# One change to the recurrence of a two-layer decoder: A blocks on half the rows of the matrix array, one head at a time

## The chip, the core and the metric

The kernel runs on one core of a Trainium2 chip. Five engines work side by side, each through its own list of instructions in order: TensorE (PE in the profile; its weight loads are listed apart as PEld), VectorE (DVE), ScalarE (ACT), GpSimd (POOL), and SyncE (SP), which here only issues DMA transfers. They wait for each other through semaphores. Matrix products write to PSUM, from which VectorE and ScalarE copy results to SBUF. The metric is the time of one execution in microseconds (us) on the device; lower is better.

## The reference, cut to what matters

The model has a layer with an RWKV-7 mixer and an MLP, shared keys and values, and a second layer with forgetting attention and an MLP, on 1024 tokens of width 1024, all in float32. The change is in the recurrence of the RWKV-7 mixer, which the reference writes token by token for each of 16 heads with 64 features:

```python
    def step(S, inp):
        r_t, w_t, k_t, v_t, kk_t, b_t = inp
        sa = jnp.einsum('bhvk,bhk->bhv', S, -kk_t)
        S = (S * w_t[:, :, None, :] + sa[..., None] * b_t[:, :, None, :]
             + v_t[..., None] * k_t[:, :, None, :])
        y_t = jnp.einsum('bhvk,bhk->bhv', S, r_t)
        return S, y_t
    ...
    mean = jnp.mean(y, axis=-1, keepdims=True)
    var = jnp.mean(jnp.square(y - mean), axis=-1, keepdims=True)
    y = (y - mean) * lax.rsqrt(var + GN_EPS)
    ...
    bonus = jnp.sum(r_h * k_h * r_k.astype(f32), axis=-1, keepdims=True) * v_h
    y = (y + bonus.reshape(B, T, D)).astype(h.dtype) * g
    return y @ w_o
```

## The kernel before, in words

The kernel does the recurrence in 16 chunks of 64 tokens. Within a chunk everything is a matrix product; between chunks only the state goes on. The 16 heads are 8 pairs, with one head of a pair on partitions 0 to 63 and the other on 64 to 127. An earlier stage scales kk, r, b and k with the decays and writes them to DRAM, by chunk (`d_KR`, `d_BK`).

What a chunk needs:

- *A blocks* (`rec_blocks`). For each head, the products of b and k (64 tokens each) with kk and r (64 tokens each) over the head's 64 features, masked to the causal part. `BK[:, p]` holds b and k of pair p, both heads, on 128 partitions. `KRz` holds kk and r of the pair so that the columns of one head are zero on the other head's partitions. One product per pair of 128 x 128 weights with 256 columns then gives the blocks of both heads. Two pairs fill a PSUM tile `ap`; VectorE multiplies it with the mask into `AE` (L416). There are four such tiles in a chunk. TensorE shows a float32 product as two weight loads and two matmuls, so four products are eight records.
- *Token-major b and k* (`rec_turn`): eight transposes into two tiles `tp`, copied by ScalarE to `BKt` (L425).
- *Inverse of the triangular system* (`rec_load_blocks`, `rec_corner`, `rec_corner2`): diagonal blocks are loaded (`B11`, `BT2`, `TT`), and the corner is made by the small products `op` and `op2`. `rec_corner` also writes kk, scaled to the chunk before, to `AE` (VectorE, L444) and scales r in place (GpSimd, L444).
- *Solve, state, output* (`rec_solve`, `rec_state`, `rec_out`): `pp` (from AE and Z, which holds the state beside v), copied to `Ps` by ScalarE; `yp` starts the output with r and the state; `sa`, scaled into Z by VectorE (L475); `u` gives the next state (VectorE L489, GpSimd `St` L494); a second `yp` adds the rest of the output.
- *Norm and gate* (`rec_norm`, `rec_gate`): VectorE takes `m` (L517, L518) and `Y` (L519) from `yp`, ScalarE the squares, and so on; one chunk later the product `zp` and the gate follow.

Chunk c does its solve, state and output, while the A blocks, transposes and corner of chunk c + 1 are made in between: part "a" of `prepare` (the first half of the A blocks) before `rec_state`, part "b" (the second half, and the transposes) after `rec_out`. From chunk 3 on, `fill` puts 24 products of the output projection (`wo`) into each chunk. In the first chunks `hook` puts in the last product of the gate (`gp`) and the loads and splits of w_o.

What sets the order: TensorE takes the recurrence's products in the order of the program (`Pinned`). The other engines' lists are made at build time by a scheduler that simulates the program, and may stand in another order than the code.

Buffers that matter: `ap`, `tp`, `op`, `op2` and `zp` share the PSUM pool `psA`, which has three buffers, taken in turn; a tile waits until the one three before it has been read. The A blocks of part "b" and the two `tp` follow each other, so the second `tp` waits for the copy of the first `ap` tile of part "b". `KRz` has two places (even and odd chunks), `BK` has one: the load of the next BK waits for the transposes of the present one.

Of the kernel before, what the change touches and what calls it, by code (L numbers as in the profile page):

```python
# [8 lines left out]
F32 = mybir.dt.float32  # L9
# [7 lines left out]
P = 128  # L17
# [12 lines left out]
# the recurrence's start: chunk of the first load of x; steps of the gate's product at each of its places;  # L30
# first place of a load of w_o, places between two loads, places from a load to its split
# [9 lines left out]
# engines of the steps where one stage follows another (v: VectorE, s: ScalarE, p: GpSimd), tile by tile.  # L41
# mlp_in (m), queries and keys (q): normalised x by tokens (n), its blocks from PSUM (r), the parts' forms (t, w.f),
# high parts (h) and low parts (l); products of rows (o: mlp_out, w: attention's w_o): the first and the last eighth
# of the rows (0, 9), parts of both sides (a, b), forms (f); ENG_O: the rows between
# [31 lines left out]
class K:  # L76
    """State shared by the stages."""
# [17 lines left out]
def rsqrt_small(k, pool, out, x, scale, eps, tag=""):  # L95
    """out = (x * scale + eps) ** -0.5 for a small tile, refined by one Newton step."""
# [20 lines left out]
def load_cols(k, a, pool, ps, which):  # L117
    """Feature vectors as columns: k.col[name] is [128, 8]."""
# [47 lines left out]
def rwkv_keep(k):  # L166
    """What lives from the projections to the recurrence."""
# [27 lines left out]
def block_tiles(k):  # L195
    """Diagonal blocks of the next two head pairs, one to a partition."""
    k.Nb = k.pi.tile([P, 32, 32], F32, tag="Nb", name="Nb", bufs=2)
# [6 lines left out]
def prep_unit(k, p, hf):  # L204
    """Half the tokens of a head pair: decays, scaled kk, r, b, k to DRAM, inverses of A_ab's diagonal blocks."""
# [16 lines left out]
    # log decay, its sum within a chunk, the exponentials about the middle of the chunk  # L222
# [26 lines left out]
    # b before k for the first head of the pair, k before b for the second  # L249
# [7 lines left out]
    # norms of kk: 1 / max(sum of squares, 1e-24); two chunks at a time  # L257
# [13 lines left out]
    # -A_ab, transposed; its diagonal 32 x 32 blocks one to a partition  # L271
# [19 lines left out]
def prep_inverse(k, b):  # L291
    """Inverses of 128 unit lower triangular 32 x 32 blocks, one on each partition."""
# [16 lines left out]
def rec_pools(k, ctx, a):  # L309
# [8 lines left out]
    k.KRz, k.TT = [], []  # L318
    for i in range(2):
        with tc.issue_after(k.gate_end.ins) if i else nullcontext():  # L320
            kr = k.rz.tile([P, NK, 2, 2, C], F32, tag=f"KRz{i}", name=f"KRz{i}")
            nc.gpsimd.memset(kr, 0.0)
            k.KRz.append(kr)
            tt = k.rc.tile([P, NK, 2, C], F32, name=f"TT{i}")
            nc.gpsimd.memset(tt, 0.0)
            k.TT.append(tt)
    # mask of an A block: rows (b | k) i, columns (kk / r, t): kk where i < t, r where i <= t
# [13 lines left out]
    # scale of the state from one chunk's reference to the next one's  # L341
# [6 lines left out]
class Pinned:  # L348
    """Matrix products that the tensor engine takes in the order of the program."""
# [14 lines left out]
def rec_values(k, c):  # L364
    """[state, v] of the first head of each pair, [v, state] of the second; the state comes from the chunk before."""
# [10 lines left out]
def rec_load(k, c):  # L376
    """Chunk c of all heads: scaled kk and r, b and k."""
    nc, w = k.nc, k.rw
    KR, TT = k.KRz[c % 2], k.TT[c % 2]
    BK = k.rc.tile([P, NK, 2, C], F32, tag="BK", name="BK")  # L380
    B11 = k.rc.tile([P, NK, 32], F32, tag="B11", name="B11")
    BT2 = k.rc.tile([P, NK, 32], F32, tag="BT2", name="BT2")
    for h in range(2):
        nc.sync.dma_start(KR[HALF[h], :, h], k.d_KR[c, HALF[h]])
# [6 lines left out]
def rec_load_blocks(k, s):  # L391
    """The triangular inverses' blocks."""
# [17 lines left out]
def rec_blocks(k, s, p2):  # L410
    """The A blocks of two head pairs."""
    ap = k.psA.tile([P, 2, 256], F32, tag="psA", name="ap")
    for j in range(2):
        p = 2 * p2 + j
# [1433 lines left out]
```

## Time and profile before

| | |
|---|---|
| runs | 2953.9, 2958.09 and 2966.1 us, median 2958.09 |
| the profiled execution | span 2954.2 us from its first to its last instruction; no time of its own beside the span is given |
| busy share of the span | PE 91%, PEld 74%, DVE 76%, ACT 40%, POOL 50% |
| mean granted TensorE clock | 0.952 |
| the recurrence | its first A block starts at 523.6 us, its last solve (`pp`) at 834.8 us |
| A blocks (`ap`, L355) | 256 matmul records, 66.7 us busy |
| masking of A blocks (`AE`, L416) | 64 VectorE instructions, 42.4 us busy |

A row of the timeline has start, duration, engine, line, operation, output <- inputs, shape, and count where equal instructions follow each other; the brackets give the idle time of the engine before it and what ended it. TensorE's matmuls overlap: a row's duration runs to the end of the last one, and the start of the next row tells when TensorE was free for it. A row of the groups has the count, the busy time of the group (overlaps counted once) and the mean duration of one.

### The profile page before, as it was taken

The page shows a single profiled execution, that of the slowest core. Times are in us where ns is not written, and L with a number is a line of the kernel's source. Part 1 is how long each engine was busy: PE and PEld are TensorE (multiplying, and loading weights), DVE is VectorE, ACT ScalarE, POOL GpSimd, SP SyncE. Part 2 cuts the span into 40 slices and gives each one's busy share as a digit, 9 for nine tenths or more (in the row PEclk, how much of TensorE's full clock was granted, in tenths as well). Part 3 has the DMA queues.
Part 4 walks back from the last instruction along what each step waited for, and adds up shares of the span by engine and source line. Part 5 has one row for each costly group of instructions (what it writes and reads, how often), then busy time and mean ns, then how long its engine had stood idle before and what let it go on. Part 6 is the DMA issues. An engine that isn't in the chain of part 4 may idle for free.

```text
span 2954.2 us, 46747 instructions
## 1 busy us (share of the span) xinstructions
PE 2675.9 (91%) x17666; PEld 2171.7 (74%) x17666; DVE 2246.8 (76%) x3496; ACT 1191.8 (40%) x2243; POOL 1478.3 (50%) x1059
## 2 busy tenths in 40 slices
PE   7998788799998999899977899999986999989998
PEld 4776676677886888677766899766665788867876
DVE  7059998677768555789998868566689755599998
ACT  5364433422243333323334434467635333323431
POOL 2055553465556554565665322333266555466555
PEclk9998888999998999999998999999998999999999
DMA  3358574665412333533102222644330333342311
GB/s 115 142 177 250 162 210 116 192 167 136 116 45 80 113 107 100 199 114 114 58 15 87 93 80 79 188 123 133 87 122 8 100 107 115 129 163 93 115 58 57
DMA packets 345457, 344.63 MB, mean 117 GB/s; under 512 B 137648, under 2 KB 274080, under 8 KB 345232
## 3 DMA queue, kind: packets, MB, share of 16 engines
q1 hardware_dynamic: 344240, 339.48, 36.8%
q8 instruction: 139, 2.28, 0.3%
q0 software_dynamic: 992, 2.17, 0.2%
q14 instruction: 86, 0.70, 0.1%
HBM read 236.59 MB, written 104.99 MB: 116 GB/s over the span
## 4 chain that ended last, share of the span: by engine, by line
PE 44%; DVE 17%; issue 4%; DMA 2%; POOL 1%; ACT 1%; SPq 0%; DVEq 0%; POOLq 0%; ACTq 0%
PE mm L355 8%; PE mm L740 6%; PE mm L739 6%; PE mm L741 6%; DVE ol L706 5%; PE mm L1333 4%; PE mm L1334 4%; PE mm L1332 3%; DVE xt L1345 3%; PE s L355 3%; PE tp L358 2%; PE o L355 2%; DVE T L1303 1%; DVE xlT L706 1%; DVE T L1314 1%
## 5 line engine op out<-in xcount | busy, mean ns | idle before, releaser
L1333 PE MATMUL mm<-ol,oh 128*128 128x512 f32 x992 | 400.4, 406 | 47.2 <-DVE ol L706 40.2
L1334 PE MATMUL mm<-oh,ol 128*128 128x512 f32 x992 | 385.1, 405 | 15.2 <-DVE ol L706 14.9
L1332 PE MATMUL mm<-oh 128*128 128x512 f32 x992 | 365.5, 401 | 27.8 <-ACT oh L703 18.7
L1333 PEld LDWEIGHTS mm<-ol,oh 128*128 128x128 f32 x992 | 193.5, 195 | 103.7 <-DVE ol L706 54.5
L1199 POOL TENSOR_TENSOR z<-z 128x512 f32<-128x512 f32 x128 | 144.7, 1131 | 205.3 <-ACT z L1198 205.3
L1332 PEld LDWEIGHTS mm<-oh 128*128 128x128 f32 x992 | 191.5, 194 | 75.2 <-ACT oh L703 21.7
L1334 PEld LDWEIGHTS mm<-oh,ol 128*128 128x128 f32 x992 | 192.9, 196 | 62.3 <-DVE ol L706 22.9
L703 ACT CAST oh<-r 128x512 fp32r<-128x512 f32 x211 | 124.0, 619 | 249.8 <-PE mm L1333 192.8
L740 PE MATMUL mm<-xlT,ah 128*128 128x512 f32 x512 | 203.7, 398 | 17.1 <-DVE xlT L706 17.0
L739 PE MATMUL mm<-xhT,ah 128*128 128x512 f32 x512 | 202.4, 397 | 5.6 <-ACT xhT L703 4.6
L741 PE MATMUL mm<-xhT,al 128*128 128x512 f32 x512 | 202.3, 396 | 0.0
L706 DVE TENSOR_TENSOR ol<-r,oh 128x512 fp32r<-128x512 f32 x193 | 190.4, 1016 | 6.9 <-ACT oh L703 2.9
L1345 DVE TENSOR_TENSOR xt<-xt,mm 128x512 f32<-128x512 f32 x288 | 181.5, 676 | 7.0 <-PE mm L1334 6.9
L703 ACT CAST ah<-w 128x512 fp32r<-128x512 f32 x125 | 77.3, 621 | 177.8 <-PE mm L740 173.0
L706 POOL TENSOR_TENSOR ol<-r,oh 128x512 fp32r<-128x512 f32 x63 | 98.7, 1571 | 97.5 <-ACT oh L703 81.4
L739 PE MATMUL mm<-xhB,ah 128*128 128x512 f32 x368 | 144.1, 391 | 0.0
L740 PE MATMUL mm<-xlB,ah 128*128 128x512 f32 x368 | 143.9, 391 | 0.0
L741 PE MATMUL mm<-xhB,al 128*128 128x512 f32 x368 | 143.1, 391 | 0.0
L703 ACT CAST oh<-S 128x512 fp32r<-128x512 f32 x102 | 63.0, 621 | 184.2 <-PE mm L1333 142.7
L740 PEld LDWEIGHTS mm<-xlT,ah 128*128 128x128 f32 x512 | 98.1, 192 | 41.1 <-DVE xlT L706 20.3
L706 DVE TENSOR_TENSOR ol<-S,oh 128x512 fp32r<-128x512 f32 x102 | 112.7, 1109 | 16.6 <-ACT oh L703 12.4
L706 POOL TENSOR_TENSOR ol<-T,oh 128x512 fp32r<-128x512 f32 x58 | 93.9, 1622 | 51.1 <-ACT oh L703 32.2
(522 smaller groups left out, 7815.7 us busy)
## 6 DMA issues: line engine op xcount, KB each, us to landing
w<-in_mlp_w_in_dram SPq DMA_DIRECT2D x64, 512.0 KB
r<-d_H SPq DMA_DIRECT2D x64, 512.0 KB
r<-in_mlp_w_out_dram SPq DMA_DIRECT2D x64, 512.0 KB
d_H<-z SPq DMA_DIRECT2D x60, 512.0 KB
raw<-in_rwkv_w_rkv_dram SPq DMA_DIRECT2D x24, 512.0 KB
d_KR<-KR SPq DMA_DIRECT2D x16, 512.0 KB
KRz<-d_KR SPq DMA_DIRECT2D x32, 256.0 KB
BK<-d_BK SPq DMA_DIRECT2D x16, 512.0 KB
```

The lines of the kernel that those rows point to most:

```text
L355: return self.tc.keep_in_program_order(self.tc.nc.tensor.matmul(*args, **kw))
L358: return self.tc.keep_in_program_order(self.tc.nc.tensor.transpose(*args))
L703: nc.scalar.copy(hi, src)
L706: lo_eng.tensor_tensor(lo, src, hi.bitcast(F32), op=ALU.subtract)
L739: te.matmul(out, ah, bh, start=i == 0, stop=False)
L740: te.matmul(out, ah, bl, start=False, stop=False)
L741: te.matmul(out, al, bh, start=False, stop=i == n - 1)
L1199: nc.gpsimd.tensor_tensor(dst, dst, dst, op=ALU.mult)
L1332: te.matmul(banks[t], ah[:, ts], bh, start=i == 0, stop=False)
L1333: te.matmul(banks[t], ah[:, ts], bl, start=False, stop=False)
L1334: te.matmul(banks[t], al[:, ts], bh, start=False, stop=i == n - 1)
L1345: nc.vector.tensor_tensor(d, d, o, op=ALU.add)
```

## The change: half-row products, no padding, two places for b and k

Each head's A block becomes a product of its own: 64 rows (the head's partitions) with 128 weight columns and 128 moving columns. The two heads of a pair alternate, and go to two PSUM tiles, one for each head. `rec_blocks` now makes four pairs at once: two `ap` tiles of four pairs by one head, where there were two tiles of two pairs by two heads. The padded `KRz` becomes a tile of the same size that holds kk and r in its first half and b and k in its second, so that b and k have two places as well; the fills with zeros fall away, and kk and r come with one transfer of 512 KB in place of two of 256 KB. The product of r and the state (`yp` of `rec_solve`) takes 64 rows in place of 128. Comments and docstrings are taken out too, which moves line numbers by a few.

```diff
-    k.KRz, k.TT = [], []
+    k.KRB, k.TT = [], []
     for i in range(2):
         with tc.issue_after(k.gate_end.ins) if i else nullcontext():
-            kr = k.rz.tile([P, NK, 2, 2, C], F32, tag=f"KRz{i}", name=f"KRz{i}")
-            nc.gpsimd.memset(kr, 0.0)
-            k.KRz.append(kr)
+            kr = k.rz.tile([P, 2, T], F32, tag=f"KRz{i}", name=f"KRz{i}")
+            k.KRB.append([kr[:, j].rearrange("p (c b t) -> p c b t", b=2, t=C) for j in range(2)])
...
-    KR, TT = k.KRz[c % 2], k.TT[c % 2]
-    BK = k.rc.tile([P, NK, 2, C], F32, tag="BK", name="BK")
+    (KR, BK), TT = k.KRB[c % 2], k.TT[c % 2]
...
-    for h in range(2):
-        nc.sync.dma_start(KR[HALF[h], :, h], k.d_KR[c, HALF[h]])
+    nc.sync.dma_start(KR, k.d_KR[c])
     nc.sync.dma_start(BK, k.d_BK[c])
...
-def rec_blocks(k, s, p2):
-    ap = k.psA.tile([P, 2, 256], F32, tag="psA", name="ap")
-    for j in range(2):
-        p = 2 * p2 + j
-        k.pe.matmul(ap[:, j], s["BK"][:, p], s["KR"][:, p], start=True, stop=True)
-    k.nc.vector.tensor_tensor(s["AE"][:, 2 * p2:2 * p2 + 2].rearrange("p c h k t -> p (c h k t)"),
-                              ap.rearrange("p c f -> p (c f)"), k.mask.rearrange("p c k t -> p (c k t)"), op=ALU.mult)
+def rec_blocks(k, s, p4):
+    aps = [k.psA.tile([P, 4, 2, C], F32, tag="psA", name="ap") for _ in HALF]
+    for j in range(4):
+        for ap, hs in zip(aps, HALF):
+            k.pe.matmul(ap[:, j], s["BK"][hs, 4 * p4 + j], s["KR"][hs, 4 * p4 + j], start=True, stop=True)
+    for h, ap in enumerate(aps):
+        k.nc.vector.tensor_tensor(s["AE"][:, 4 * p4:4 * p4 + 4, h], ap, k.mask, op=ALU.mult)
...
-                eng.tensor_tensor((AE, KR)[i][hs, :, h, i], KR[hs, :, h, i], sc, op=ALU.mult)
+                eng.tensor_tensor((AE[hs, :, h, 0], KR[hs, :, 1])[i], KR[hs, :, i], sc, op=ALU.mult)
...
-                k.pe.matmul(yp[hs, p], s["KR"][:, p, h, 1, :], Z[:, p, h, :], start=p == 0, stop=False)
+                k.pe.matmul(yp[hs, p], s["KR"][hs, p, 1, :], Z[hs, p, h, :], start=p == 0, stop=False)
...
             if "a" in parts:
                 rec_blocks(k, s, 0)
                 hook()
+                hook()
+            if "b" in parts:
                 rec_blocks(k, s, 1)
                 hook()
-            if "b" in parts:
-                rec_blocks(k, s, 2)
-                hook()
-                rec_blocks(k, s, 3)
                 hook()
                 rec_turn(k, s, 0)
                 hook()
```

How the order of the instructions moves is shown at three places. The first is TensorE in a chunk in the middle of the recurrence, before (KRz is kk and r, BK is b and k, and ap is an A block):

```order
L355 MATMUL pp<-Z,AE 64x64 x16
L355 MATMUL yp<-Z,KRz_4508 64x64 x16
L355 MATMUL sa<-Ps,TT_4510 64x64 x16
L355 MATMUL ap<-KRz_4512,BK 128x256 x4
L355 MATMUL u<-Z,BKt 64x64 x16
L355 MATMUL yp<-Z,AE 64x64 x16
L355 MATMUL ap<-KRz_4512,BK 128x256 x4
L358 MATMUL tp<-ident,BK 128x128 x8
```

And TensorE in the same chunk now:

```order
L354 MATMUL pp<-Z,AE 64x64 x16
L354 MATMUL yp<-Z,KRz_4508 64x64 x16
L354 MATMUL sa<-Ps,TT_4509 64x64 x16
L354 MATMUL ap<-KRz_4511 128x128 x8
L354 MATMUL u<-Z,BKt 64x64 x16
L354 MATMUL yp<-Z,AE 64x64 x16
L354 MATMUL ap<-KRz_4511 128x128 x8
L357 MATMUL tp<-ident,KRz_4511 128x128 x8
```

The order of the groups is the same; each group of A blocks is eight products of 128 columns in place of four of 256.

The second place is VectorE's list in such a chunk, from the solution Z to the variance, before:

```order
L475 TENSOR_TENSOR Z_5740<-sa_6055,ns2_96 64x8x64 x2
L416 TENSOR_TENSOR AE_6002<-ap_6074,mask_4516 128x512
L416 TENSOR_TENSOR AE_6002<-ap_6078,mask_4516 128x512
L489 TENSOR_TENSOR Z_6014<-u_6082,St_5827 64x8x64 x2
L517 TENSOR_REDUCE m_6144<-yp_6038 128x8
L518 TENSOR_SCALAR m_6144<-m_6144 128x8
L416 TENSOR_TENSOR AE_6002<-ap_6120,mask_4516 128x512
L519 TENSOR_TENSOR Y_6143<-yp_6038,m_6144 128x512
L416 TENSOR_TENSOR AE_6002<-ap_6124,mask_4516 128x512
L523 TENSOR_REDUCE var_6150<-ysq_6148 128x8
```

And now:

```order
L472 TENSOR_TENSOR Z_5766<-sa_6087,ns2_96 64x8x64 x2
L414 TENSOR_TENSOR AE_6034<-ap_6106,mask_4514 128x4x128
L414 TENSOR_TENSOR AE_6034<-ap_6107,mask_4514 128x4x128
L486 TENSOR_TENSOR Z_6046<-u_6118,St_5857 64x8x64 x2
L514 TENSOR_REDUCE m_6184<-yp_6070 128x8
L515 TENSOR_SCALAR m_6184<-m_6184 128x8
L516 TENSOR_TENSOR Y_6183<-yp_6070,m_6184 128x512
L414 TENSOR_TENSOR AE_6034<-ap_6156,mask_4514 128x4x128
L414 TENSOR_TENSOR AE_6034<-ap_6157,mask_4514 128x4x128
L520 TENSOR_REDUCE var_6190<-ysq_6188 128x8
```

The masking of part "b" has moved: Y stood between its two instructions, and now stands ahead of both.

The third place is SyncE's list of transfers at the start of the recurrence, before (d_B and d_T are the last inverses, d_g the gate; KRz of buffer 4508 serves chunks 0 and 2, that of 4512 chunk 1; BK_4699 is b and k of chunk 1):

```order
L306 DMA d_B_105<-Tb_1213 128x1024
L305 DMA d_T_104<-Tm_1214 128x1024
L399 DMA B11_4536<-d_B_105 32x8x32 x2
L1073 DMA d_g_64<-xt0_4562 128x2x512
L401 DMA BT2_4537<-d_T_104 32x8x32 x2
L405 DMA TT0_4510<-d_T_104 32x8x32 x4
L1073 DMA d_g_64<-xt1_4580 128x2x512
L405 DMA TT1_4514<-d_T_104 32x8x32 x3
L1073 DMA d_g_64<-gs_4598 128x2x512
L405 DMA TT1_4514<-d_T_104 32x8x32
L384 DMA KRz0_4508<-d_KR_98 64x8x128
L385 DMA BK_4699<-d_BK_99 128x1024
```

And now, a little earlier in the list, from b and k of chunk 0 on (buffer 4508 again serves chunks 0 and 2, 4511 chunk 1):

```order
L382 DMA KRz0_4508<-d_BK_99 128x1024
L381 DMA KRz1_4511<-d_KR_98 128x1024
L382 DMA KRz1_4511<-d_BK_99 128x1024
L339 DMA lnw_4520<-in_rwkv_lnx_w_dram 64x8x64 x2
L339 DMA lnb_4521<-in_rwkv_lnx_b_dram 64x8x64 x2
L369 DMA Z_4539<-d_v_65 64x8x64 x2
L369 DMA Z_4719<-d_v_65 64x8x64 x2
L510 DMA Vh_4851<-d_v_65 64x8x64 x2
L1068 DMA d_g_64<-xt0_4566 128x2x512
L1068 DMA d_g_64<-xt1_4580 128x2x512
L381 DMA KRz0_4508<-d_KR_98 128x1024
L306 DMA d_B_105<-Tb_1213 128x1024
```

b and k of chunk 1 have moved from behind the loads of TT to the very start, and kk and r of chunk 2 from behind the loads of TT to ahead of d_B. Elsewhere the scheduler swaps neighbours on VectorE, ScalarE, GpSimd and SyncE at the start of both MLPs, in the middle of the first MLP's second product, and in the projection of keys and values; TensorE's order changes at some of these places too. No instruction is added or taken away there.

More of the change, by code (lines that the diff above doesn't have):

```diff
@@ L76 @@
 class K:
+    pass
 def engine(k, e):
```

## The prediction

> **What bounds the kernel now.** I read the page first, then cut the recurrence into stretches, then followed one chunk instruction by instruction. The chain that ended last begins only behind this stage, so the stage has to be read from its own windows.
>
> ```profile
> span 2954.2 us, 46747 instructions
> core 0: us, PE busy (x) PEld busy (x) DVE busy (x) ACT busy (x) POOL busy (x), PEclk, DMA share, GB/s
> 545.00:565.00 20.00, 13.57 (x223) 11.05 (x222) 9.16 (x13) 6.37 (x12) 6.81 (x5) 0.83 0.92 270
> 565.00:606.00 41.00, 32.74 (x586) 27.22 (x586) 33.94 (x45) 16.92 (x34) 37.88 (x28) 0.96 0.81 221
> 630.00:834.00 204.00, 198.91 (x3331) 165.09 (x3327) 152.24 (x278) 60.72 (x144) 115.89 (x107) 1.00 0.48 119
> ```
>
> There are three regimes. At 545 to 565 us transfers fill the DMA engines (0.92) and TensorE waits. To 606 GpSimd is the bound (37.88 of 41). From 630 to 834, eleven chunks, TensorE is busy 198.91 of 204. By that row, shorter products would pay at once. But a busy TensorE also counts the tail of a product behind which it waits, so here is a chunk of that stretch:
>
> ```profile
> 706.16 1.10 PE L355 MATMUL yp<-Z,KRz 128*64 128x64 f32 x32
> 707.09 1.10 PE L355 MATMUL sa<-Ps,TT 128*64 128x64 f32 x32
> 708.12 1.99 PE L355 MATMUL ap<-KRz,BK 128*128 128x256 f32 x8
> 710.05 1.15 PE L355 MATMUL u<-Z,BKt 128*64 128x64 f32 x32
> 711.03 1.10 PE L355 MATMUL yp<-Z,AE 128*64 128x64 f32 x32
> 712.06 1.99 PE L355 MATMUL ap<-KRz,BK 128*128 128x256 f32 x8
> 713.89 0.60 PE L358 MATMUL tp<-ident,BK 128*128 128x128 f32 x4
> 714.95 0.66 PE L358 MATMUL tp<-ident,BK 128*128 128x128 f32 x4 [0.45 <-DVE AE L416]
> 715.36 0.48 PE L355 MATMUL wo<-woh,zh 128*128 128x512 f32 x1
> ...
> 708.34 1.41 DVE L475 TENSOR_TENSOR Z<-sa,ns 64x512 f32<-64x512 f32 x2 [2.37 <-PE sa L355]
> 709.78 1.29 DVE L416 TENSOR_TENSOR AE<-ap,mask 128x512 f32<-128x512 f32 x2
> 711.25 1.41 DVE L489 TENSOR_TENSOR Z<-u,St 64x512 f32<-64x512 f32 x2 [0.18 <-PE u L355]
> 712.69 0.69 DVE L517 TENSOR_REDUCE m<-yp 128x8 f32<-128x512 f32 x1
> 713.41 0.89 DVE L518 TENSOR_SCALAR m<-m 128x8 f32<-128x8 f32 x1
> 714.21 0.68 DVE L416 TENSOR_TENSOR AE<-ap,mask 128x512 f32<-128x512 f32 x1
> 714.81 0.68 DVE L519 TENSOR_TENSOR Y<-yp,m 128x512 f32<-128x512 f32 x1
> 715.41 0.68 DVE L416 TENSOR_TENSOR AE<-ap,mask 128x512 f32<-128x512 f32 x1
> ...
> 712.09 2.18 POOL L494 TENSOR_TENSOR St<-Z,sc 64x512 f32<-64x512 f32 x2
> ```
>
> The reader should see two things. The first group of A blocks (708.12) stands where TensorE has to wait for VectorE's Z anyway: Z ends at 708.34 + 1.41 = 709.75, and u starts at 710.05. Behind the second group (712.06) the second tp waits for the first AE of that group, which ends at 714.21 + 0.68 = 714.89, because VectorE has Z, m and m ahead of it. So VectorE ends both groups' stretches, not the products. A second kind of chunk has a short m (it ends early, where in the first it runs until GpSimd's St ends at 714.27):
>
> ```profile
> 750.95 0.22 DVE L518 TENSOR_SCALAR m<-m 128x8 f32<-128x8 f32 x1
> 751.08 0.68 DVE L416 TENSOR_TENSOR AE<-ap,mask 128x512 f32<-128x512 f32 x1
> 751.43 1.04 PE L358 MATMUL tp<-ident,BK 128*128 128x128 f32 x8
> 752.22 0.48 PE L355 MATMUL wo<-woh,zh 128*128 128x512 f32 x1
> ```
>
> There tp does not wait visibly, but wo again starts 752.22 - 751.76 = 0.46 behind the end of AE; in the first kind it is 715.36 - 714.89 = 0.47.
>
> **The change part by part.** *The products.* A group takes 713.89 - 712.06 = 1.83 us for eight records of 256 columns, 0.229 each. Now it is sixteen records of 128 columns. That two products on half the rows run side by side, these rows show:
>
> ```profile
> L355 PE MATMUL s<-K,Q 64*128 64x512 f32 x96 | 24.6, 508 | 0.0
> 224.25 1.15 PE L277 MATMUL np__1541<-KR,BK 64*64 64x64 f32 x32
> ```
>
> 96 records of 508 ns are 48.8 us laid end to end, and 24.6 are counted: they overlap in pairs, on 64 rows and 128 columns. np uses the same b and kk by heads and halves, in float32. So a group should take 16 x 0.115 / 2 = 0.92 us, 0.91 less; two groups in 16 chunks make 29 us of TensorE work saved. Bounds: 0.92 if pairs overlap, 1.83 if none does. I take 0.92, the row of the same shape.
>
> *What of it reaches the end, first group.* u can start no earlier than Z allows, 0.30 sooner than now, and VectorE's second Z idles only 0.18 for u. So the gain is 0.18 per chunk (bounds 0 and 0.30).
>
> *Second group.* VectorE now takes m, m, Y, AE, AE. Y needs m: it starts at 713.41 + 0.89 + 0.03 = 714.33 (0.03 is the step from 712.69 + 0.69 to 713.41, between dependent instructions) and ends at 715.01. AE starts 0.08 before that (as Y now overlaps AE, 714.89 against 714.81) and ends at 715.61 in place of 714.89. The second tp waits for it, and wo starts 0.72 later. In the short-m chunk: m ends at 751.17, Y at 751.88, AE at 752.48 in place of 751.76, again 0.72. TensorE gets to tp 0.91 earlier and waits longer. This is a loss of 0.72 per chunk (bounds: 0.60, Y's step alone from 714.81 to 715.41, and 0.89, if Y also waits for a longer m). Later work has slack: op needs the last AE, which ends where it did within 0.12, and stands behind six wo.
>
> *yp on half the rows*, between pp and sa, which both use all rows: the array changes its form twice more. One change is priced by sa to ap, 708.12 - 707.09 = 1.03, against yp to sa, 0.93: 0.10 each. A wait of sa for Ps hides it in five chunks of eleven:
>
> ```profile
> PEld sa L355 <- ACT Ps L464: 3.7, 5, 0.9
> ```
>
> So 2 x 0.10 x 6/11 = 0.11 per chunk (bounds 0 and 0.4, twice the whole tail of 0.2 that a product's last record has behind the next one's start). The Trainium skill, "TensorEngine Tiling (Array Packing)", Key Properties, says that changing the tiling mode drains TensorE. In the rows ap starts at 708.12, before the recorded end of sa at 708.19, so a full drain is not seen here; by the rule the cost would be the upper bound, 0.4, and the sum some 2 us higher.
>
> *Start of the recurrence.* Today chunk 1 waits for its b and k:
>
> ```profile
> 547.67 1.22 PE L355 MATMUL sa<-Ps,TT 128*64 128x64 f32 x32 [0.69 <-ACT Ps L464]
> 553.78 3.50 PE L355 MATMUL ap<-KRz,BK 128*128 128x256 f32 x8 [4.89 <-issue]
> 557.21 1.15 PE L355 MATMUL u<-Z,BKt 128*64 128x64 f32 x32
> 548.39 0.58 SPq L385 DMA_DIRECT2D BK<-d_BK  x1
> 548.93 1.41 DVE L475 TENSOR_TENSOR Z<-sa,ns 64x512 f32<-64x512 f32 x2 [9.29 <-PE sa L355]
> 558.04 1.32 POOL L407 TENSOR_TENSOR B<-B,ns 32x256 f32<-32x256 f32 x2 [15.38 <-DMA B<-d_B]
> ```
>
> BK is issued at 548.39 and ap runs at 553.78. With its own place BK comes at the start, ap follows sa, and u can start behind Z's end, 548.93 + 1.41 = 550.34, nearly 7 us earlier. But SyncE now takes kk and r of chunk 2 ahead of d_B, and that transfer waits for the last A block of chunk 0: d_B, and with it B11 and op of chunk 0, move back by 1 to 2 us. And chunk 1's op still needs B on GpSimd, which starts at 558.04 when its transfer has landed; w_o's splits now stand ahead of it. GpSimd then sets the pace to 606, so only what starts GpSimd earlier counts. The 1 MB taken out of the full stretch (b and k of chunk 1, kk and r of chunk 2), at that row's 270 GB/s, makes 3.9 us; less the 1 us of the later d_B I take 3 us gained. Bounds: 4.9, the whole wait, and a loss of 1.
>
> *What costs nothing.*
>
> ```profile
> 502.03 3.54 POOL L322 MEMSET KRz<- 128x2048 f32 x2
> ...
> 523.15 1.08 POOL L372 MEMSET Z<- 64x512 f32 x2 [10.63 <-PE mm L355]
> ```
>
> The two fills with zeros, 3.54 us, are followed by a wait of GpSimd for TensorE of 10.63, which takes them up whole. One transfer in place of two per chunk saves SyncE some 0.6 us where DMA is at 0.48. AE and the scaling of r handle as many elements as before. If VectorE were late, AE's wider step in SBUF would be the next place to look.
>
> *Other stages.* Neighbours swap at four places; nothing is added. I take 0. Each place can win or lose a couple of VectorE instructions of 0.7 to 1 us, as those above, so the bounds are 6 us either way.
>
> *Sum.* Per chunk -0.18 + 0.72 + 0.11 = +0.65; in the twelve chunks 3 to 14, where wo follows tp, +7.8. With -3 at the start: +4.8 on 2954.2. The runs' median, 2958.1, stands 3.9 above the profiled span; added to it, the forecast is 2963 us, 0.2% slower, inside the 0.5% (15 us) that a measurement of this kernel can tell from no change.
>
> **The rivals.** *The saved products count after all (faster).* For it: TensorE busy 198.91 of 204. If VectorE masked the second group at once, wo would follow the group by tp's own time: 712.06 - 0.18 + 0.92 + 0.10 + 0.79 (752.22 - 751.43) = 713.69 in place of 715.36, and 0.9 earlier in short-m chunks, about 1.2 on average. Twelve chunks make 14, and with the start 17: 2941 us. It decides where the second tp does not wait for AE. Against it: VectorE's list has Y ahead of both AE, and m starts only behind Z. The place holds for the chunks as they run today; where a chunk's m comes early enough, the wait could shrink to nothing, so I leave this rival a real share.
>
> *Half-row products do not overlap here (slower).* Each of the sixteen records loads 128 weight columns of its own for only 128 moving columns. If loads of about 0.1 us each come on top and pairs do not overlap, a group takes 16 x (0.115 + 0.1) = 3.4 us, 1.6 more than now; u and tp then come late, 3 us per chunk, 15 chunks: about 3005 us. It decides once a group outlasts the wait, at 1.9 us for the first and about 2.7 for the second. Against it stand the rows of s and np above; for it, that s shows one pair at a time, not eight in a row.
>
> *The start or the other stages decide.* A gain of 4.9 at the start, no cost of yp and the 6 us of other orders going well give 2949; all of it going badly gives 2975. Both stay inside the 0.5% or reach just beyond.
>
> **How the numbers follow.** Forecast with the third rival inside 0.5%: 0.68. Saved products count, near 2941 or somewhat below: 0.14. No overlap: 0.06. Third rival beyond 0.5%, on the slow side: 0.12, since neighbours swap in four stages that I price at nothing. As 0.5% is 15 us and 2941 is 17 below 2958, this gives faster 0.14, same 0.68, slower 0.18. The forecast's own range is 2946 to 2980: the bounds of yp (+3), Y (+2), start (+4 or -2) and other stages (6 either way). The range given, 2940 to 2982, takes in the first rival's time too, and leaves out the second rival and about half of the third's slow side.
>
> **What the profile after would show.** Right: groups of ap with sixteen records in about 0.9 us; u not more than 0.3 earlier behind sa; the second tp waiting 1.5 to 2 us for AE; wo about 5.8 to 6 behind u in long-m chunks, in place of 5.31; no idle time before ap of chunk 1. Wrong: ap groups of 1.8 us or more (no overlap); AE of the second group ending within 2.5 us of its start (then TensorE gains); yp to sa well over 1.2 us; or the recurrence shorter or longer as said and the sum lost in another stage.

## The result

The changed kernel takes 2972.4 us (median of five runs, 2970.5 to 2980.8), the kernel before 2958.3 in the runs beside it. The ratio is 1.0055, with a 95% interval of 1.0037 to 1.0072: slower by about half a per cent, 14 us between the medians. The forecast was 2963, in a range of 2940 to 2982.

The head of the page of the changed kernel, and the three stretches that the prediction showed of the kernel before (TensorE, its weight loads, VectorE, ScalarE, GpSimd, granted clock, DMA):

```profile
span 2970.6 us, 47213 instructions
PE 2674.0 (90%) x17922; PEld 2168.7 (73%) x17922; DVE 2248.6 (76%) x3496; ACT 1194.5 (40%) x2243; POOL 1472.7 (50%) x1057
```

```profile
545.00:565.00 20.00, 17.15 (x292) 14.61 (x287) 13.85 (x20) 8.76 (x18) 10.20 (x8) 0.73 0.92 258
565.00:606.00 41.00, 29.96 (x507) 25.81 (x507) 34.47 (x39) 14.06 (x27) 35.54 (x26) 0.76 0.64 186
630.00:834.00 204.00, 181.29 (x3346) 150.77 (x3342) 147.12 (x265) 56.45 (x132) 115.11 (x105) 0.99 0.46 117
```

From 630 to 834 TensorE is now busy 181.3 us of 204, where it was 198.9: there is less to do, and more waiting. From 545 to 606 us the granted clock is lower than it was, 0.73 and 0.76 in place of 0.83 and 0.96. The work itself shrank as the change says. The A blocks are 512 records, and by the view of the groups they are busy for 39.6 us in place of 66.7:

```profile
L354 PE MATMUL ap<-KRz 64*128 64x128 f32 x512 | 39.6, 297 | 0.0
```

The chunk that answers to the one in the prediction, from the timeline of TensorE, VectorE and GpSimd:

```profile
711.80 1.16 PE L354 MATMUL ap<-KRz 64*128 64x128 f32 x16
712.90 0.33 PE L354 MATMUL u<-Z,BKt 128*64 128x64 f32 x2
713.48 1.09 PE L354 MATMUL u<-Z,BKt 128*64 128x64 f32 x29 [0.26 <-DVE Z L472]
...
714.41 1.15 PE L354 MATMUL yp<-Z,AE 128*64 128x64 f32 x31
715.49 1.16 PE L354 MATMUL ap<-KRz 64*128 64x128 f32 x16
716.58 0.66 PE L357 MATMUL tp<-ident,KRz 128*128 128x128 f32 x4
718.88 0.66 PE L357 MATMUL tp<-ident,KRz 128*128 128x128 f32 x4 [1.64 <-DVE AE L414]
719.29 0.48 PE L354 MATMUL wo<-woh,zh 128*128 128x512 f32 x1
...
714.67 1.41 DVE L486 TENSOR_TENSOR Z<-u,St 64x512 f32<-64x512 f32 x2
716.11 0.69 DVE L514 TENSOR_REDUCE m<-yp 128x8 f32<-128x512 f32 x1
716.83 0.67 DVE L515 TENSOR_SCALAR m<-m 128x8 f32<-128x8 f32 x1
717.54 0.69 DVE L516 TENSOR_TENSOR Y<-yp,m 128x512 f32<-128x512 f32 x1
718.14 1.28 DVE L414 TENSOR_TENSOR AE<-ap,mask 128x512 f32<-128x512 f32 x2
...
716.42 2.18 POOL L491 TENSOR_TENSOR St<-Z,sc 64x512 f32<-64x512 f32 x2
```

The second group of A blocks starts at 715.49 and TensorE is free for tp at 716.58. The second tp then waits until 718.88, because VectorE does m, m and Y before it masks the first of the two new tiles (718.14). The waits of TensorE from 630 to 810 us, before and after (us in total, times, longest):

```profile
PE sa L355 <- ACT Ps L464: 3.0, 5, 0.7
PE tp L358 <- DVE AE L416: 2.1, 5, 0.6
```

```profile
PE tp L357 <- DVE AE L414: 13.5, 9, 2.0
PE sa L354 <- ACT Ps L461: 3.7, 5, 2.0
PE u L354 <- DVE Z L472: 2.4, 9, 0.4
```

Where in the program the 16.4 us of the two profiles lie, cut at the starts of instructions in the timeline, at the last wo at its end (chunks counted from 0; "chunk" is the mean from the solve `sa` of chunk 4 to that of chunk 14; "first U" is VectorE's first sum U of the MLP; the last column runs to the start of the last transfer of the output, some 3 us before the end of the span):

| kernel | to first ap | first ap to sa of chunk 4 | chunk | sa of chunk 14 to last wo | last wo to first U | first U to end |
|---|---|---|---|---|---|---|
| before | 523.6 | 107.8 | 18.74 | 53.3 | 40.3 | 2038.7 |
| changed | 522.3 | 108.0 | 19.63 | 52.2 | 44.2 | 2044.4 |
| difference | -1.3 | +0.3 | +0.89, x10 = +8.9 | -1.1 | +4.0 | +5.7 |

The same chunk cut into steps (means over chunks 4 to 13, from start to start):

| kernel | sa to yp of AE | to first tp | to second tp | to wo | to pp | to next sa |
|---|---|---|---|---|---|---|
| before | 3.97 | 2.86 | 0.73 | 0.40 | 8.47 | 2.30 |
| changed | 3.78 | 2.22 | 2.19 | 0.41 | 8.47 | 2.56 |

Of the shorter products, 0.19 us come through in the first group and 0.64 in the second, and 1.46 go at the second tp. The mean of the first group hides two kinds of chunk: in eight of the ten, sa to yp of AE takes 3.63 in place of 3.94 to 3.99, in chunk 6 it takes 4.00, and in chunk 5 it takes 4.75. In chunk 5 sa has waited 1.98 us for Ps, and behind that wait the granted clock is 0.57 and the A blocks take 2.01 us (from 652.76 to the start of u at 654.77) in place of 1.09:

```profile
651.08 1.75 PE L354 MATMUL sa<-Ps,TT 128*64 128x64 f32 x32 [1.98 <-ACT Ps L461]
652.76 2.08 PE L354 MATMUL ap<-KRz 64*128 64x128 f32 x16
```

```profile
651.00:655.00 4.00, 3.92 (x52) 3.58 (x54) 2.14 (x7) 0.33 (x3) 0.06 (x1) 0.57 0.58 146
```

### The profile page after: what moved, and what is told of

The parts are those of the page before. It is cut to its first block, busy times and chain, and to the rows that moved or that the text cites. A ratio compares the mean times of both kernels' runs of the same rounds, so it can differ in the third digit from the quotient of the medians.

```text
span 2970.6 us, 47213 instructions
## 1 busy us (share of the span) xinstructions
PE 2674.0 (90%) x17922; PEld 2168.7 (73%) x17922; DVE 2248.6 (76%) x3496; ACT 1194.5 (40%) x2243; POOL 1472.7 (50%) x1057
## 3 DMA queue, kind: packets, MB, share of 16 engines
q0 software_dynamic: 992, 2.17, 0.2%
## 5 line engine op out<-in xcount | busy, mean ns | idle before, releaser
L1340 DVE TENSOR_TENSOR xt<-xt,mm 128x512 f32<-128x512 f32 x288 | 181.3, 676 | 7.2 <-PE mm L1329 7.2
L735 PEld LDWEIGHTS mm<-xlT,ah 128*128 128x128 f32 x512 | 99.1, 194 | 40.3 <-DVE xlT L701 16.5
L734 PEld LDWEIGHTS mm<-xhT,ah 128*128 128x128 f32 x512 | 98.9, 194 | 34.5 <-ACT xhT L698 6.3
```

What stands on the lines that cost most here:

```text
L734: te.matmul(out, ah, bh, start=i == 0, stop=False)
L735: te.matmul(out, ah, bl, start=False, stop=False)
L1340: nc.vector.tensor_tensor(d, d, o, op=ALU.add)
```

## The experiments

All times below are medians beside runs of the kernel before on the same chip; its own medians there were 2955.0 to 2957.6. The ratios are to that kernel.

### VectorE's order, and the buffer that carries it to TensorE

Two edits to the changed kernel that each remove the wait of the second tp, one at VectorE, one at PSUM, and both together. The first puts m's scaling and Y behind the two maskings, from chunk 1 on (`rec_norm` gets the next chunk as `nxt`, for chunk 0 none):

```diff
+        last = k.nc.vector.tensor_tensor(s["AE"][:, 4 * p4:4 * p4 + 4, h], ap, k.mask, op=ALU.mult)
+    return last
...
-                rec_blocks(k, s, 1)
+                s["masked"] = rec_blocks(k, s, 1)
...
-    nc.vector.tensor_scalar_mul(m, m, 1.0 / C)
-    nc.vector.tensor_tensor(Y, yp, m.unsqueeze(2).broadcast_to(S3), op=ALU.subtract)
+    with k.tc.issue_after(nxt["masked"].ins) if nxt else nullcontext():
+        nc.vector.tensor_scalar_mul(m, m, 1.0 / C)
+        nc.vector.tensor_tensor(Y, yp, m.unsqueeze(2).broadcast_to(S3), op=ALU.subtract)
```

> The changed kernel, with VectorE's order changed at one place: m's scaling and Y stand behind the two maskings (AE) of the second group of A blocks. Theory (VectorE's order behind the second group makes the loss): the second tp no longer waits 1 to 1.8 us for AE but about 0.3; wo starts 0.9 us earlier behind u in chunks with a short m and 1.5 earlier in those with a long one, 1.2 on average, in twelve chunks 14 us: 2958 us, level with the kernel before. Rival (the loss is the change of the array's form and other stages; the wait for AE only moves on to op): 2968 us or more, with op waiting where tp waited.

Measured: 2957.8 us, ratio 0.9997 (0.9988 to 1.0007). The waits of its TensorE, 630 to 810 us:

```profile
PE sa L354 <- ACT Ps L462: 5.5, 5, 1.5
PE tp L357 <- DVE AE L414: 3.4, 10, 0.3
```

13.5 us of waiting for AE have become 3.4, 0.3 each, and a chunk lasts 18.53 us. No wait of op has come in its place. So VectorE's order, with Y and m's scaling ahead of the maskings, carries the loss in these chunks. The edit puts both behind them, where the kernel before had m's scaling ahead and Y between, so it takes away somewhat more than the change had put there; a chunk is 0.2 us shorter than before the change.

The second edit leaves that list alone and takes `tp` from the other pool:

```diff
-    tp = k.psA.tile([P, 4, P], F32, tag="psA", name="tp")
+    tp = k.psC.tile([P, 4, P], F32, tag="psC", name="tp")
```

> The changed kernel, with the two tp tiles taken from the pool of pp, sa and u (psC), so that they wait for no masking; VectorE's order stays, Y ahead of AE. Theory (it is the buffer of psA that carries VectorE's order to TensorE): no wait in the second tp, wo starts 5.0 us behind u in place of 6.3, twelve chunks 14 us: 2958 us. Rival (the last AE ends at 6.5 us behind u whatever tp does, and op waits for it behind six wo): op waits, the gain is under 4 us: 2968 us or more.

Measured: 2951.8 us, ratio 0.9983 (0.9969 to 0.9997); a chunk of 18.51 us. The second tp starts 0.49 behind the first, in place of 2.19. The rival was partly right: from wo to pp 9.21 us pass in place of 8.47, since op now waits for the last AE in some chunks and its copies come later. It did not hold for the total, which was better than either theory said.

> The changed kernel, with both edits: maskings ahead of m's scaling and Y, and tp in the pool of pp, sa and u. Theory: neither tp nor op waits, 1.4 us per chunk, 17 us: 2955 us. Rival (array form and other stages): 2968 us or more.

Measured: 2957.3 us, ratio 1.0005 (0.9994 to 1.0015). This missed: with neither wait, a chunk takes 18.86 us, more than with either edit. The timeline of ScalarE and TensorE at the end of a chunk shows where it went:

```profile
725.25 1.06 ACT L589 ACTIVATE zl<-xt 128x1024 fp32r<-128x1024 f32 x1 [1.92 <-DVE xt L586]
...
726.42 0.58 ACT L462 COPY Ps<-pp 128x512 f32<-128x512 f32 x1
...
723.10 1.15 PE L354 MATMUL pp<-Z,AE 128*64 128x64 f32 x32
...
727.06 1.15 PE L354 MATMUL sa<-Ps,TT 128*64 128x64 f32 x32 [1.74 <-ACT Ps L462]
```

In every second chunk the square of x stands ahead of the copy Ps in ScalarE's list, and it waits for VectorE's last addition of `wo`. TensorE reaches sa sooner and waits there: 10.0 us in this stretch, up to 2.7 at once. This is the next limit behind AE. A part of the loss is the granted clock: behind the two longest of these waits (2.70 and 2.45 us, in chunks 5 and 7) it was 0.50 from 649.4 to 656.2 us and 0.51 from 690.3 to 693.8, and from sa to yp of AE these chunks took 5.75 and 4.67 us, where chunks 9, 11 and 13 took 4.23.

The same edit of `tp` on the kernel before:

> The kernel before, with the tp tiles in the pool of pp, sa and u. Theory: only the chunks with a long m have a wait to lose, 0.5 to 0.8 us in half of twelve chunks, 4 us: 2954 us. Rival (the shorter products count as soon as the wait for AE is gone): the changed kernel with the same edit is then faster than this one by 0.4 us per chunk in the recurrence; if the products do not count, the two recurrences last the same.

Measured: 2961.0 us, ratio 1.0010 (1.0000 to 1.0020), no gain where 4 us were expected. Tp lost its wait (0.44 from the first to the second in place of 0.73), but in chunks 5 and 7 sa waits for Ps instead (1.84 and 2.17 us): pp to sa 2.59 in place of 2.30. Behind it, in chunk 5, u waits for Z (0.68 and 0.40); in chunk 7 the granted clock was 0.61 from 690.9 to 695.3 us, and the A blocks took 3.15 us in place of 1.9. So sa to yp of AE takes 4.26 on average in place of 3.97. A wait taken away in one place came back in another. Against the changed kernel with this edit, the recurrence is 0.5 us per chunk slower; how much of that is the products, this pair does not tell.

### Do the half-row products run side by side, and does their length count?

In the changed kernel, the four products of one head are put ahead of the four of the other, so that neighbours use the same rows:

```diff
-    for j in range(4):
-        for ap, hs in zip(aps, HALF):
+    for ap, hs in zip(aps, HALF):
+        for j in range(4):
```

> The changed kernel with the half-row products of a group in another order: four of one head, then four of the other, so that neighbours use the same rows. VectorE's list then has the first AE of the second group ahead of Y again. Theory (alternation is what makes them overlap, but VectorE sets the wait behind the second group): a group takes 1.8 us in place of 1.1, and still the chunk gets shorter, 18.8 us in place of 19.6, since tp waits for an AE that ends 0.7 us sooner: 2962 us. Rival (the length of the products counts): chunks of 20 us or more, 2976 us. Second rival (they overlap in any order): a group of 1.1 us.

Measured: 2956.9 us, ratio 1.0003 (0.9993 to 1.0012), a chunk of 18.96 us. Its timeline:

```profile
713.16 1.71 PE L354 MATMUL ap<-KRz 64*128 64x128 f32 x16
714.80 0.65 PE L357 MATMUL tp<-ident,KRz 128*128 128x128 f32 x4
716.11 0.66 PE L357 MATMUL tp<-ident,KRz 128*128 128x128 f32 x4 [0.66 <-DVE AE L414]
...
715.38 0.68 DVE L414 TENSOR_TENSOR AE<-ap,mask 128x512 f32<-128x512 f32 x1
715.98 0.67 DVE L516 TENSOR_TENSOR Y<-yp,m 128x512 f32<-128x512 f32 x1
716.58 0.67 DVE L414 TENSOR_TENSOR AE<-ap,mask 128x512 f32<-128x512 f32 x1
```

A group takes 714.80 - 713.16 = 1.64 us, where alternating heads take 1.09 (715.49 to 716.58). So alternation is what overlaps them. And with the longer products a chunk is 0.67 us shorter, because the scheduler puts the first AE ahead of Y again. That is the clearest sign that VectorE, not the products, ended this part of the chunk. Of the 15 us between the totals of the two kernels only some 7 lie there; 10 lie behind the first U, where the two do not differ in code.

Once the waits are gone, does the length count? For this a third edit takes the square of x from ahead of Ps:

```diff
-                    if e == 1 and tt < NK - 1:
-                        ss = k.rw.tile([P, 1], F32, tag="ssx", name="ssx")
-                        nc.scalar.activation(zl.rearrange("p a b -> p (a b)"), xt[tt], AF.Square, accum_out=ss)
-                        rsqrt_small(k, k.rw, k.rstd[tt], ss, 1.0 / D, 1e-6, tag="x")
+                    if e == 1 and tt < NK - 1:
+                        late.append(tt)
...
+        def squares(after=None, mask=None):
+            while late:
+                tt = late.pop(0)
+                ss = k.rw.tile([P, 1], F32, tag="ssx", name="ssx")
+                with tc.issue_after(after.ins) if after else nullcontext():
+                    nc.scalar.activation(zs[tt][1].rearrange("p a b -> p (a b)"), xt[tt], AF.Square, accum_out=ss)
+                with tc.issue_after(mask.ins) if mask else nullcontext():
+                    rsqrt_small(k, k.rw, k.rstd[tt], ss, 1.0 / D, 1e-6, tag="x")
...
+            squares(ps, nxt["masked"] if more else None)
```

Here `ps` is the copy Ps of the present chunk; the call stands behind part "b". First with the edit of `tp` alone:

> The changed kernel with tp in the pool of pp, sa and u, and the square of x, which stands ahead of the copy Ps on ScalarE in every second chunk, put behind it (its small follow-up on VectorE behind the maskings). Theory (without the wait for AE, sa's wait for Ps is the next limit): from pp to sa 2.2 us in every chunk in place of 2.2 and 2.6 in turn; op still waits for the last AE; chunks of 18.1 us in place of 18.5: 2948 us. Rival (another wait takes its place): 18.5 us, 2952 us.

Measured: 2945.3 us, ratio 0.9963 (0.9950 to 0.9975), a chunk of 17.67 us, better than expected: pp to sa takes 2.21 us on average, and op waits less than it did. Then with all three edits, on the changed kernel and on the kernel before:

> The changed kernel with all three edits: maskings ahead of m's scaling and Y, tp in the pool of pp, sa and u, the square of x behind Ps. Theory: from sa to pp 15.2 us, from pp to sa 2.2, chunks of 17.4 to 17.8 us in place of 19.6: 2941 us. Rival (GpSimd or VectorE is the next limit): chunks of 18.3 us or more, 2952 us.

> The kernel before with the same three edits: full-row A blocks of 1.8 us, and no wait for AE or Ps. Theory (once the waits are gone, the length of the A blocks counts): from sa to pp 16.1 us, from pp to sa 1.9, chunks of 18.0 us, 0.6 more than the changed kernel with the three edits; 2948 us against 2941. Rival (the products never count): chunks as long as those of the changed kernel with the three edits.

Measured: 2948.9 us, ratio 0.9971 (0.9959 to 0.9982), and 2953.1 us, ratio 0.9989 (0.9979 to 0.9999). The waits of TensorE from 630 to 810 us, in the changed kernel with the three edits and in the kernel before with them:

```profile
PE u L354 <- DVE Z L473: 2.8, 11, 0.3
PE sa L354 <- ACT Ps L462: 1.7, 3, 0.9
```

```profile
PE sa L355 <- ACT Ps L464: 1.0, 4, 0.4
```

A chunk takes 17.56 us with half-row products and 18.24 with full ones: 0.68 less, near the 0.6 expected. So the products' saving does count, once tp no longer waits for the maskings. By steps, sa to yp of AE takes 3.63 in place of 3.98 and from there to the first tp 2.23 in place of 2.88; pp to sa takes 2.39 in place of 2.12, with the changes of form (below) and a little more waiting for Ps. In the total it is 4 us between medians, and the intervals overlap; in the recurrence, with one profile of each kernel, it is plain. Both totals missed what was expected (2941 and 2948), and the changed kernel with three edits is not faster than with the two of the run before.

### The array's form

The kernel before, with only the first `yp` on half the rows:

```diff
-                k.pe.matmul(yp[hs, p], s["KR"][:, p, h, 1, :], Z[:, p, h, :], start=p == 0, stop=False)
+                k.pe.matmul(yp[hs, p], s["KR"][hs, p, h, 1, :], Z[hs, p, h, :], start=p == 0, stop=False)
```

> The kernel before, with only the first yp (r times the state) on 64 rows, read from the padded tile; A blocks and transfers stay. Theory (a change of the array's form costs about 0.1 us each way): from pp to sa 2.16 us in place of 1.92 in the chunks in which sa does not wait for Ps, no change where it waits, 0.12 us per chunk on average: 2960 us. Rival (changes cost nothing, the 2.16 of the changed kernel come from its A blocks): 1.92 us as before, 2958 us. Second rival (the array drains at each change): 0.4 us or more in each chunk, 2964 us.

Measured: 2958.1 us, ratio 1.0010 (1.0001 to 1.0019). The timeline of a chunk in which sa does not wait, in the kernel before and in this one:

```profile
779.50 1.15 PE L355 MATMUL pp<-Z,AE 128*64 128x64 f32 x32
780.48 1.10 PE L355 MATMUL yp<-Z,KRz 128*64 128x64 f32 x32
781.42 1.10 PE L355 MATMUL sa<-Ps,TT 128*64 128x64 f32 x32
```

```profile
784.26 1.15 PE L355 MATMUL pp<-Z,AE 128*64 128x64 f32 x32
785.34 1.15 PE L355 MATMUL yp<-Z,KRz 64*64 64x64 f32 x32
786.42 1.15 PE L355 MATMUL sa<-Ps,TT 128*64 128x64 f32 x32
```

From pp to sa 2.16 us in place of 1.92: 0.24 for the two changes of form, as in the changed kernel; over chunks 4 to 13, with those in which sa waits, 2.41 in place of 2.30. The Trainium skill, "TensorEngine Tiling (Array Packing)", Key Properties, says that a change of the tiling mode drains TensorE. These rows show 0.24 us for the two changes, under the 0.4 that the prediction set as the upper bound for both; yp starts at 785.34, before the recorded end of pp (784.26 + 1.15 = 785.41), so a full drain is not seen here either.

### The start, and a tile that moved

Two runs on what else the change moved. First an unused tile where BK used to be, so that the next stage's tiles lie as before:

```diff
+    k.rc.tile([P, NK, 2, C], F32, tag="BK", name="spare")
     nc.sync.dma_start(KR, k.d_KR[c])
```

> The changed kernel with an unused tile of 4 KB per partition in the place that the old BK had in its pool, so that the tiles of the next stage lie where they lay before. In the changed kernel the eighth xhB cast of the MLP's start waits 6.7 us for the last wo, in the kernel before none does, and from the last wo to the first U 44.2 us pass in place of 40.3. Theory (the removed BK moved the next stage's tiles onto the weights of w_o): 40.3 us again, no wait of xhB, 3.9 us less: 2968 us. Rival (the order of the lists makes it): 44.2 us again, 2972 us.

Measured: 2972.0 us, ratio 1.0055 (1.0039 to 1.0072). ScalarE's timeline at the start of the MLP, in the changed kernel and in this one:

```profile
868.21 3.73 ACT L698 CAST xhB<-raw 128x512 fp32r<-128x512 f32 x7
878.65 0.62 ACT L698 CAST xhB<-raw 128x512 fp32r<-128x512 f32 x1 [6.71 <-PE wo L354]
```

```profile
871.66 4.26 ACT L699 CAST xhB<-raw 128x512 fp32r<-128x512 f32 x8
```

The eighth cast no longer waits for the last wo, and the stage from the last wo to the first U takes 40.6 us in place of 44.2. So the places of the tiles make this loss: with BK gone, the last of the casts has to wait until the last wo has been done, and with an unused tile of that size it has not. The total did not follow, since the start of the recurrence (110.5 in place of 108.0), the chunks (19.73) and the rest (2047.4 in place of 2044.4) were longer in this kernel. What of that is the new layout and what is one execution, these runs don't tell.

Then b and k in one place again, in a tile of that size:

```diff
-    (KR, BK), TT = k.KRB[c % 2], k.TT[c % 2]
+    (KR, _), TT = k.KRB[c % 2], k.TT[c % 2]
+    BK = k.rc.tile([P, NK, 2, C], F32, tag="BK", name="BK")
```

> The changed kernel with b and k of a chunk in one place again, in a tile of the size and pool that it had before; kk and r stay in the new tile. Theory (the second place gains 3 to 4 us at the start, which the changed order of VectorE hides in the changed kernel's sum): from the first A block to the solve of chunk 4 111.5 us in place of 108.0; the MLP's start as before the change (40.3 us): 2972 us. Rival (the second place gains nothing): 108 us, 2968 us.

Measured: 2963.9 us, ratio 1.0028 (1.0018 to 1.0038). By stages the theory holds: 112.8 us to chunk 4 in place of 108.0, and the wait for BK is back at the A blocks of chunk 1:

```profile
552.96 2.08 PE L354 MATMUL ap<-KRz,BK 64*128 64x128 f32 x16 [3.60 <-DMA BK<-d_BK]
```

The MLP's start takes 40.3 us. Yet the total is 8 us under what was expected, as the part from the first U to the end took 2036.2 us, 8 less than in the changed kernel. That part has no code of the change in it, and over all these kernels it lies between 2034.2 and 2047.4.

### A version that is faster than both

The three edits and the unused tile together:

> The changed kernel with all three edits and the unused tile in the place of the old BK. Theory: as with the three edits alone, and 40.3 us in place of 44.2 from the last wo to the first U: 2937 us. Rival (what the stage gains is lost elsewhere, as in the changed kernel with the unused tile alone): level with the three edits alone.

Measured: 2943.9 us, ratio 0.9955 (0.9943 to 0.9968), the fastest of all, though its interval overlaps those of the two kernels before it without the tile. The MLP's start is at 40.3 us as expected; the chunks (17.76) and the last solve to the last wo (54.5 in place of 52.9) give most of it back.

The stages of all kernels, as in the table above:

| kernel | median us | first ap to sa of chunk 4 | chunk | last wo to first U | first U to end |
|---|---|---|---|---|---|
| before | 2958.3 | 107.8 | 18.74 | 40.3 | 2038.7 |
| changed | 2972.4 | 108.0 | 19.63 | 44.2 | 2044.4 |
| maskings first | 2957.8 | 104.8 | 18.53 | 44.2 | 2041.0 |
| tp in psC | 2951.8 | 103.8 | 18.51 | 44.2 | 2038.5 |
| both | 2957.3 | 103.6 | 18.86 | 44.2 | 2042.8 |
| heads apart | 2956.9 | 109.0 | 18.96 | 44.2 | 2034.2 |
| spare tile | 2972.0 | 110.5 | 19.73 | 40.6 | 2047.4 |
| one place for BK | 2963.9 | 112.8 | 19.93 | 40.3 | 2036.2 |
| tp in psC, square later | 2945.3 | 103.1 | 17.67 | 44.2 | 2037.3 |
| all three | 2948.9 | 104.9 | 17.56 | 43.9 | 2039.6 |
| all three, spare tile | 2943.9 | 104.9 | 17.76 | 40.3 | 2039.6 |
| before, tp in psC | 2961.0 | 108.6 | 19.02 | 40.6 | 2039.4 |
| before, half-row yp | 2958.1 | 111.9 | 18.81 | 40.3 | 2040.0 |
| before, all three | 2953.1 | 107.7 | 18.24 | 40.6 | 2035.4 |

## Why the prediction was right, and where it was not

The mechanism in the steady chunks was right, and nearly the size. The time fell inside the range, but 9 us above the forecast. The forecast said no change beyond 0.5%, with 0.12 for the third rival's slow side; the result is a loss of about 0.5%, whose interval (0.37 to 0.72%) lies on both sides of that line. Of the 16.4 us between the two profiles the recurrence's ten chunks hold 8.9. The start and the other stages hold 7.6, where -3 was forecast, so that the time lies in the range owes as much to the width of the range as to the mechanism.

- *First group.* Forecast -0.18 per chunk, measured -0.19 (3.97 to 3.78). That these agree so well is luck: in eight of ten chunks the gain was 0.31 to 0.36, at the upper bound of 0.30 or just beyond it, while chunk 6 lost 0.06 and chunk 5 0.69, at the lower clock shown above. In the chunk shown u starts 2.18 behind sa (712.90 - 710.72) in place of 2.96, not the 0.3 sooner at most that was forecast; its first two records no longer wait for the end of Z, and the rest waits for the second half of Z (0.26 in the row at 713.48).
- *Second group.* Forecast +0.72, measured 2.22 + 2.19 + 0.41 - (2.86 + 0.73 + 0.40) = +0.83. The runs with maskings first and with tp in psC, of which the first cuts this wait to 0.3 us and the second removes it, and which each shorten the chunk by 1.1, show that it is this wait.
- *yp on half the rows.* Forecast +0.11, measured +0.26 (2.30 to 2.56). The price of a change of form was right (0.24 for two, where sa does not wait). The sa of chunk 5 waited 1.98 for Ps, the longest in the row of waits, 1.6 more than in its like; spread over ten chunks that is the missing 0.15.
- *Products.* Forecast 0.92 per group, measured 1.09. The reading of s, 48.8 us laid end to end and 24.6 counted, did not show pairs by itself, since the records of the full-row A blocks also overlap (256 x 404 ns = 103 us, 66.7 counted); the run with heads apart shows them. The error was harmless here, as TensorE waits for VectorE behind both groups.
- *The start.* Forecast -3, measured +0.3. The step that failed is the count "in the twelve chunks 3 to 14": the same order of Y and AE stands in chunks 0 to 2 too, and costs more there, because m takes longer there (1.18, 2.02 and 2.30 us, later 0.17 to 1.00). The waits of TensorE for AE from 545 to 606 us, in the kernel before, the changed one and the one with maskings first:

```profile
PE tp L358 <- DVE AE L416: 1.3, 2, 0.8
```

```profile
PE tp L357 <- DVE AE L414: 9.8, 3, 4.6
```

```profile
PE tp L357 <- DVE AE L414: 5.1, 3, 3.2
```

  The gain of the second place for BK is there: with the order mended (maskings first, tp in psC, both) this part takes 103.6 to 104.8 us, 3 to 4 less than before; with one place it takes 4.8 more than in the changed kernel. The lower granted clock of this part (0.73 and 0.76) does not decide it: with tp in psC it is as low (0.68 and 0.75), and the part is 4.2 us shorter.
- *Other stages.* Forecast 0, bounds 6 either way; measured -1.3 - 1.1 + 4.0 + 5.7 = +7.3, beyond the bound. "Neighbours swap at four places; nothing is added" failed: the smaller pool also moved tiles, and a cast of the MLP's start got a wait of 6.7 us for the last wo (the run with the spare tile shows it). The prediction went by the order of the lists and not by the places in SBUF. The other 5.7 us, from the first U on, are not explained: the part varies by 13 us over kernels that do not touch it, and the changed kernel's is among the longest. A low granted clock goes with a long part: by the clock's records in the traces, it stood at a half for 154.8 us of this part in the kernel before, 168.7 in the changed one, 175.3 where the part is longest (2047.4), and 144.6 to 154.8 in the three kernels where it is shortest (2034.2 to 2036.2). Whether the clock is cause or consequence, these runs do not tell.
- *The first rival* (the saved products count) was wrong for this kernel and right about what decides it: where the second tp does not wait, half-row products are worth 0.68 us per chunk.
- *The second rival* (no overlap) fell: 16 records in 1.09 us.
- *The sums of the range.* The lower ends do not follow from the bounds: with the start's -2 and the other stages' -6, 2963 gives 2955 and not 2946; with a start of 4.9, no cost of yp and -6, 2963 - 1.9 - 1.3 - 6 gives 2954 and not 2949. A cost of 0.4 for the form in twelve chunks would add 3.5 us, as in the range, and not 2. The time came out on the other side, so nothing hung on it.

## What to carry to other kernels

Before pricing a shorter product, ask which engine takes its result and what stands ahead of that in its list: here a saving of 0.7 us per group (1.83 to 1.09) became a loss of 0.9 per chunk, for the most part because one instruction of 0.7 us changed places. Compare not only the order of each engine's list but also where tiles lie, since a tile that is dropped from a pool can give a later stage a new wait. When one wait is removed, look for the next one on the same path (AE, then Ps) before judging the change itself.

## What the runs showed of the hardware

VectorE's scaling of m, eight columns, took 2.30 us in chunk 2 of the changed kernel, and ended when GpSimd's split of w_o ended (598.26 + 2.67 = 600.93; 598.65 + 2.30 = 600.95). The maskings behind it held the second tp for 4.63 us:

```profile
598.65 2.30 DVE L515 TENSOR_SCALAR m<-m 128x8 f32<-128x8 f32 x1
600.99 0.69 DVE L516 TENSOR_TENSOR Y<-yp,m 128x512 f32<-128x512 f32 x1
...
598.26 2.67 POOL L566 TENSOR_TENSOR wol<-woraw,woh 128x1024 fp32r<-128x1024 f32 x1
...
602.34 1.11 PE L357 MATMUL tp<-ident,KRz 128*128 128x128 f32 x4 [4.63 <-DVE AE L414]
```

In the chunk at 716 us, m (716.83 + 0.67 = 717.50) ends with the first of the two St (716.42 + 2.18 / 2 = 717.51). The Trainium skill, "SBUF — State Buffer", SBUF: two separate sides, says that GpSimd and some kinds of VectorE instructions share a pair of ports, which the one that starts first holds to its end while the other is blocked. Both rows agree with that. Y, which ran beside the second of the two St, took 0.69 us as in chunk 2. So an instruction of eight columns can take as long as the GpSimd instruction beside it.

Half-row products of the two halves overlapped when they alternated: 16 records took 1.09 us when heads alternate and 1.64 when they do not, a factor of 1.5, not 2.

The granted clock fell to about a half for some us at a time, and TensorE's products then took nearly twice as long: the A blocks of chunk 5 in the changed kernel took 2.01 us (652.76 to 654.77) at a clock of 0.57, where others took 1.09. In this stretch it came behind waits of sa of 1.98, 2.17, 2.45 and 2.70 us, and not behind those of 1.74 and 1.84. With the spare tile it also came (0.50 from 641.0 to 644.4 us) where no wait of sa was above 0.5, behind a wait of tp of 1.78. So the rows show the two together, and not that such a wait alone causes it.
